# Two transformer blocks on one core: the attention norm through Ln and Exp, lambda as a scalar operand, squares in PSUM, and two buffers for the branches of layer 0

## The chip, the cores and the metric

The kernel runs on one core of a Trainium2 chip. The core's engines run side by side, each through its own queue in order: TensorE (PE, with its weight loads as PEld), VectorE (DVE), ScalarE (ACT), GpSimd (POOL) and SyncE (SP), which here issues most of the DMA transfers. They wait for one another through semaphores. On-chip data lies in SBUF, matmul results in PSUM. The metric is the time of one execution on the device in microseconds (us); lower is better.

## The reference

The first block has two layers, on 512 tokens and 256 tokens of context, with a model width of 2048 and 8 heads. Each layer makes shift, scale and gate vectors from c, projects the modulated tokens by w_in, and runs three kinds of branches: differential attention with a norm of its own, a short convolution, and an average over windows of 2, 4, 8 or 16 tokens less the token itself, which goes through a small matrix. Their concatenation goes through w_out, a residual and a layer norm. A second block (banded attention and a convolution of width 31) follows; the change does not touch it. The part that matters:

```python
def _diff_attn(qb, k_all, v_all, lam):
    s = jnp.einsum('bqhid,bkhid->bhiqk', qb * ATTN_SCALE, k_all)
    p = jax.nn.softmax(s, axis=-1)
    a = p[:, :, 0] - lam * p[:, :, 1]
    return jnp.einsum('bhqk,bkhe->bqhe', a, v_all)

def _diff_subln(o, g, lam_init):
    y = o * lax.rsqrt(jnp.mean(jnp.square(o), axis=-1, keepdims=True) + RMS_EPS) * g * (1.0 - lam_init)
    return y.reshape(o.shape[0], o.shape[1], D_ATTN)

def _short_conv(u, b_gate, c_gate, g, w):
    v = c_gate * u
    vp = jnp.pad(v, ((0, 0), (1, 1), (0, 0)))
    y = vp[:, :T] * w[0] + vp[:, 1:T + 1] * w[1] + vp[:, 2:] * w[2]
    return jax.nn.silu(g) * (b_gate * y)

def _multiscale_pool(u, g, pool_w_l, pool_scale_l):
    ...
    y = jnp.einsum('btgc,gcd->btgd', d, pool_w_l).reshape(B, T, D_POOL) * pool_scale_l
    return jax.nn.silu(g) * y

for l in range(DEPTH):
    sh_l, sc_l, g_l = jnp.split(jax.nn.silu(c) @ w_mod[l] + b_mod[l], 3, axis=-1)
    hl = xl * (1.0 + sc_l[:, None, :]) + sh_l[:, None, :]
    parts_l = jnp.split(hl @ w_in[l], SPLIT_POINTS, axis=-1)
    ...
    xl = _layernorm(DEEPNORM_ALPHA * xl + g_l[:, None, :] * out_l, ln_g[l], ln_b[l])
```

## The kernel before

**Units.** A unit is one block of 128 output columns of w_in against all tokens: 16 steps over the width, each with three matmuls in split precision (a high and a low part of the weights, `whi` and `wlo`, and of the tokens) for the 512 tokens, and as many for the 256 of context. `mm3` (L160 to L163) issues them. SP loads a chunk of weights (`wraw`), ACT rounds it to `whi` (L156), POOL subtracts to get `wlo` (L140). A unit's two results lie in buffers of the PSUM tag `ps_m`, which has four; `ps_s`, `ps_t` and `ps_v` have one each.

**Attention** (`attention`, `attend`). Per head there are four units: Q, K, V and a gate. Q and K are rotated and split, V goes through a copy from PSUM (`vT`, L347 and L348, on ACT) and transposes; the gate becomes SG through `silu2` (a tanh on ACT at L240, a product on DVE at L241). `attend` then goes through groups of 256 queries: three in layer 0 (qp 0 and 1 are the 512 tokens, qp 2 the context), two in layer 1. For each half group and each of the two maps: scores in `ps_s` (L381), maximum (DVE, L386), exp with its sum (ACT, L393), reciprocal of the sum (L395). Then the two maps are combined with lambda (L398 to L401) and transposed through `ps_t` (L408), with a high and a low copy (aTh by ACT, L412, aTl by DVE, L413). The product with V lands in `ps_v` (L418), DVE multiplies it into SG (L422), and for the norm it is squared, split and summed over the partitions by a matmul with ones (L424 to L432). Its result `ms` is copied to `rt` (L435 or L438); after qp 1, for 512 columns, and after qp 2, for 256, Sqrt (ACT, L440), reciprocal (DVE, L445), the product with SG (L446) and the store follow. An activation function needs its table on ACT; where the function changes to one of another table, the built program has an ACT_TABLE_LOAD ahead of it, under the line of that activation.

**Side work.** `dots` (L779 to L815) computes products of modulation weights with c. Every unit advances it by some steps (`along`, `advance`), recorded at a lower priority. A piece `gw` of 512 columns is loaded by SP and used twice, for the tokens and for the context. A product either is one instruction on DVE (L809) or, where `pool_every` picks it, a product on POOL (L805) and a sum on ACT (L806). All of them write their product to the one buffer of the tag `gj`. In layer 0's attention all products go by POOL and ACT; in the branches all 128 go by DVE, with four `gw` buffers.

**Branches** (`conv_tile`, `pool_tile`). Layer 0 runs conv 0, pool 0, conv 1, pool 1, conv 2, pool 2, pool 3, conv 3; the side work runs from pool 0 on. A conv tile takes four units; V and yc are its padded input and its result, stored at L523. A pool tile sums shifted copies of U on POOL (S), takes the mean less the token (dd, L550 and L551), splits dd into dh (ACT, L554) and dl (POOL), and sends them through a matrix into `ps_v`. V and U share the tag "V"; yc, dd and the result y share the tag "yc"; each tag has one buffer.

**Order.** The kernel is written in the Tile framework, which puts in the waits; a scheduler sets the order of the instructions on each engine, on the grounds of data, buffers and priorities. So an edit in one place can move instructions elsewhere.

## Time and profile before

| | us |
|---|---|
| median of 3 runs | 3560.86 (3556.08 to 3561.03) |
| the profiled execution, its own time | 3560.77 |
| its span | 3559.0 |
| PE busy | 3295.3 (93% of the span) |
| DVE busy | 2289.7 (64%) |
| POOL busy | 1956.4 (55%) |
| ACT busy | 1518.4 (43%) |

The profile is of one execution. Its views cut it in several ways. The windows give, for a stretch of time, the busy time of every engine and the mean clock granted to PE, as a share of full speed. The waits give, engine by engine, what it waited for: in front of the arrow the instruction that waits, behind it the one that released it, then the sum in us, how often, and the longest. The timeline lists instructions by start; in brackets stands how long the engine was idle before one and what ended that. The lines group all instructions of one line, engine and shape: count, busy us in all, mean ns of one, then the idle time before them and what ended it. An engine's idle time costs something only where PE, or whatever else sets the end, waits for it.

### The profile page before, as it was taken

The numbers are of one execution on the slowest core, as the hardware profiler recorded it, in microseconds if no ns is written. First come the engines' busy times: TensorE is split into PE (matmuls) and PEld (weight loads), VectorE is DVE, ScalarE is ACT, GpSimd is POOL, SyncE is SP. The second block draws the span as 40 slices with busy tenths as digits, with TensorE's granted clock in tenths as the row PEclk, the third lists the DMA queues.
The fourth block names the chain that finished last, engine by engine and source line by source line (L and its number), as shares of the span: only waits on it lengthen the run. The fifth ranks groups of instructions, "written<-read, shape, count | busy, mean of one in ns | idle before, by whom it ended". The sixth has DMA issues, their size and how long they took to land. (4 is left out here: it accounts for less than half of the span.)

```text
span 3559.0 us, 48355 instructions
## 1 busy us (share of the span) xinstructions
PE 3295.3 (93%) x16850; PEld 2782.2 (78%) x16850; DVE 2289.7 (64%) x3489; ACT 1518.4 (43%) x3181; POOL 1956.4 (55%) x1436
## 2 busy tenths in 40 slices
PE   8898998898998998999999999998999899999997
PEld 7787887787887786778888888877768677787765
DVE  6845555555468548674555564585577799986576
ACT  2256666655431122243666654322445333345333
POOL 2356776665234543256787763587776344444432
PEclk8799999999999999999999999999999999999998
DMA  8744333332245447664555542586775222223575
GB/s 322 284 130 122 104 106 106 98 107 81 68 150 188 143 144 215 188 224 137 154 151 153 162 122 86 204 303 221 230 229 189 74 92 80 86 77 110 180 225 190
DMA packets 274148, 554.70 MB, mean 156 GB/s; under 512 B 30992, under 2 KB 40048, under 8 KB 265712
## 3 DMA queue, kind: packets, MB, share of 16 engines
q1 hardware_dynamic: 271344, 539.04, 47.1%
q0 software_dynamic: 2560, 12.58, 1.7%
q8 instruction: 132, 2.16, 0.3%
q14 instruction: 112, 0.92, 0.1%
HBM read 510.69 MB, written 28.23 MB: 151 GB/s over the span
## 5 line engine op out<-in xcount | busy, mean ns | idle before, releaser
L163 PE MATMUL ps_m<-h,whi 128*128 128x512 f32 (+1 forms) x4736 | 1614.8, 398 | 50.2 <-ACT vT L347 35.1
L140 POOL TENSOR_TENSOR wlo<-wraw,whi 128x512 fp32r<-128x512 f32 x768 | 1119.4, 1474 | 946.6 <-ACT whi L156 882.4
L163 PEld LDWEIGHTS ps_m<-h,whi 128*128 128x128 f32 x4736 | 898.3, 192 | 237.4 <-ACT vT L347 37.4
L156 ACT CAST whi<-wraw 128x512 fp32r<-128x512 f32 x1040 | 607.0, 618 | 874.0 <-DMA wraw<-in_w_out_dram 285.9
L163 PE MATMUL ps_m<-h,wlo 128*128 128x512 f32 (+1 forms) x2368 | 937.5, 396 | 0.6 <-POOL wlo L140 0.6
L163 PE MATMUL ps_m<-hc,whi 128*128 128x256 f32 x2048 | 557.0, 283 | 0.9 <-DVE SG L241 0.9
L805 POOL TENSOR_TENSOR gpr<-gw,gv 128x512 f32<-128x512 f32 x320 | 426.0, 1331 | 220.3 <-ACT gpr L806 149.4
L163 PEld LDWEIGHTS ps_m<-h,wlo 128*128 128x128 f32 x2368 | 453.7, 192 | 94.5 <-POOL wlo L140 2.0
L163 PEld LDWEIGHTS ps_m<-hc,whi 128*128 128x128 f32 x2048 | 383.1, 190 | 4.6 <-DVE SG L241 1.4
L140 DVE TENSOR_TENSOR wlo<-wraw,whi 128x512 fp32r<-128x512 f32 x272 | 239.2, 893 | 202.9 <-ACT whi L156 202.6
L806 ACT ACTIVATE gpr<-gpr 128x512 f32<-128x512 f32 x320 | 201.8, 631 | 271.9 <-POOL gpr L805 270.0
L163 PE MATMUL ps_m<-hc,wlo 128*128 128x256 f32 x1024 | 289.1, 282 | 0.0
L989 DVE SCALAR_TENSOR_TENSOR acc<-gu,pack,acc 128x511 f32<-128x511 f32 (+24 forms) x240 | 230.3, 972 | 5.4
L609 PE MATMUL ps_m<-wlo,y 128*128 128x512 f32 x512 | 205.5, 402 | 18.1 <-POOL wlo L140 10.9
L809 DVE SCALAR_TENSOR_TENSOR gpr<-gw,gv 128x512 f32<-128x512 f32 x232 | 214.3, 924 | 8.7 <-DMA gw<-in_w_ada_dram 1.6
L386 DVE TENSOR_REDUCE nb<-ps_s 128x1 f32<-128x768 f32 (+1 forms) x160 | 135.2, 845 | 114.5 <-PE ps_s L381 113.3
L610 PE MATMUL ps_m<-whi,y 128*128 128x512 f32 x512 | 202.6, 397 | 2.5 <-DVE y L140 2.3
L163 PEld LDWEIGHTS ps_m<-hc,wlo 128*128 128x128 f32 x1024 | 194.5, 190 | 0.8
L608 PE MATMUL ps_m<-whi,y 128*128 128x512 f32 x512 | 181.8, 397 | 6.5 <-ACT whi L156 5.4
L413 DVE TENSOR_TENSOR aTl<-ps_t,aTh 128x384 fp32r<-128x384 f32 (+1 forms) x144 | 77.6, 539 | 166.8 <-ACT aTh L412 166.4
L282 DVE SCALAR_TENSOR_TENSOR wm<-wm,ca 128x2048 f32<-128x2048 f32 x50 | 128.8, 2575 | 21.0 <-DMA wm<-in_w_ada_dram 11.6
L381 PE MATMUL ps_s<-K,Q 128*128 128x384 f32 x576 | 133.9, 346 | 8.3 <-ACT E L393 6.6
(351 smaller groups left out, 5217.9 us busy)
## 6 DMA issues: line engine op xcount, KB each, us to landing
wraw<-in_w_in_dram SPq DMA_DIRECT2D x640, 256.0 KB, 2.9
wraw<-in_w_out_dram SPq DMA_DIRECT2D x384, 256.0 KB, 3.4
wm<-in_w_mod_dram SPq DMA_DIRECT2D x48, 1024.0 KB, 6.0
gw<-in_w_mod_dram SPq DMA_DIRECT2D x192, 256.0 KB, 3.4
gw<-in_w_ada_dram SPq DMA_DIRECT2D x136, 256.0 KB, 3.3
wm<-in_w_ada_dram SPq DMA_DIRECT2D x14, 1024.0 KB, 5.9
K<-K POOLq DMA_DIRECT2D x32, 384.0 KB, 5.4
gv<-in_cc_dram SPq DMA_DIRECT2D x40, 256.0 KB, 3.6
```

Source lines behind the costliest of these rows:

```text
L140: eng.tensor_tensor(lo, src, hi.bitcast(F32), op=ALU.subtract)
L156: nc.scalar.copy(hi[:, sl], raw)
L163: nc.tensor.matmul(ps, w, mv[part], start=(first and p == 0), stop=(last and p == 2))
L381: nc.tensor.matmul(o, Qm[:, q0:q0 + 128], kp[:, c * ncol:(c + 1) * ncol], start=i == 0, stop=i == 1)
L386: nc.vector.reduce_max(nb, sv, axis=AX.XY, negate=True)
L608: nc.tensor.matmul(ps, yh, hi[:, sl], start=(k == 0), stop=False)
L609: nc.tensor.matmul(ps, yh, lo[:, sl], start=False, stop=False)
L610: nc.tensor.matmul(ps, yl, hi[:, sl], start=False, stop=(k == KT - 1))
L805: nc.gpsimd.tensor_tensor(pr, w, t, op=ALU.mult)
L806: nc.scalar.activation(pr, pr, AF.Copy, scale=scale, accum_out=part[v][:, i:i + 1])
L809: nc.vector.scalar_tensor_tensor(junk, w, scale, t, op0=ALU.mult, op1=ALU.mult, accum_out=part[v][:, i:i + 1])
L989: nc.vector.scalar_tensor_tensor(A[:, s:], U[:, :NL - s], wj(i), A[:, s:], op0=ALU.mult, op1=ALU.add)
```

## The change

- The product of the reciprocal sum with minus lambda, one column, takes lambda as a scalar operand (`tensor_scalar`) in place of a second tensor.
- The squares `o2` go to the second half of the PSUM bank that holds `o`, in place of an SBUF tile.
- The norm: ACT reads `ms` from PSUM with Ln (scale 8 and the same bias), into `rt`, for each group; then Exp with scale -0.5 follows where Sqrt was, for 512 or 256 columns. Copy, Sqrt and DVE's reciprocal are gone; the product with SG stays.
- In layer 0 (l = 0) the tags "V" and "yc" have two buffers (`2 - l`); in layer 1 they keep one.
- The dots in the branches of layer 0 have three `gw` buffers in place of four, and every third product goes by POOL and ACT, in all 43 of 128.

```diff
@@ -395,7 +395,7 @@
                     nc.vector.reciprocal(r, d)
                     es.append(e)
                     ds.append(r)
-                nc.vector.tensor_tensor(ds[1], ds[1], neglam[l], op=ALU.mult)
+                nc.vector.tensor_scalar(ds[1], ds[1], neglam[l], None, op0=ALU.mult)
                 E0, E1 = es
                 nc.vector.tensor_scalar(E0, E0, ds[0], None, op0=ALU.mult)
                 nc.vector.scalar_tensor_tensor(E0, E1, ds[1], E0, op0=ALU.mult, op1=ALU.add)
@@ -420,7 +420,7 @@
                     )
             y = SG[:, qp * 256:(qp + 1) * 256]
             nc.vector.scalar_tensor_tensor(y, o, subg[l], y, op0=ALU.mult, op1=ALU.mult)
-            o2 = ap_.tile([128, 256], F32, name="o2", tag="o2", bufs=1)
+            o2 = ov[:, 256:]
             nc.scalar.square(o2, o)
             o2h = ap_.tile([128, 256], F32R, name="o2h", tag="o2h", bufs=1)
             o2l = ap_.tile([128, 256], F32R, name="o2l", tag="o2l", bufs=1)
@@ -430,20 +430,18 @@
             ms = msv[:, :256]
             nc.tensor.matmul(ms, ones_r, o2h, start=True, stop=False)
             nc.tensor.matmul(ms, ones_r, o2l, start=False, stop=True)
+            if qp != 1:
+                rt = ap_.tile([128, 512], F32, name="rt", tag="rt", bufs=1)
+            r = slice(256, 512) if qp == 1 else slice(0, 256)
+            nc.scalar.activation(rt[:, r], ms, AF.Ln, bias=eps_t, scale=8.0)
             if qp == 0:
-                rt = ap_.tile([128, 512], F32, name="rt", tag="rt", bufs=1)
-                nc.scalar.copy(rt[:, :256], ms)
                 continue
-            r = slice(256, 512) if qp == 1 else slice(0, 256)
-            nc.scalar.copy(rt[:, r], ms)
             n = 512 if qp == 1 else 256
-            nc.scalar.activation(rt[:, :n], rt[:, :n], AF.Sqrt, bias=eps_t, scale=8.0)
+            nc.scalar.activation(rt[:, :n], rt[:, :n], AF.Exp, scale=-0.5)
             for i in range(n // 256):
                 q0 = (0, 256)[i] if qp == 1 else 512
-                ri = rt[:, i * 256:(i + 1) * 256]
                 y = SG[:, q0:q0 + 256]
-                nc.vector.reciprocal(ri, ri)
-                nc.vector.tensor_tensor(y, y, ri, op=ALU.mult)
+                nc.vector.tensor_tensor(y, y, rt[:, i * 256:(i + 1) * 256], op=ALU.mult)
             o = 0 if qp == 1 else 512
             nc.sync.dma_start(Yd[4 + h][:, o:o + n], SG[:, o:o + n])
 
@@ -497,9 +495,9 @@
         uu = xa.tile([128, T], F32, name="uu", tag="uu", bufs=1)
         for o, vo, n in seqs:
             nc.scalar.copy(uu[:, o:o + n], pt(u, o))
-        V = xa.tile([128, T + 4], F32, name="V", tag="V", bufs=1)
+        V = xa.tile([128, T + 4], F32, name="V", tag="V", bufs=2 - l)
         u = unit(w, 8 + j, H, cx)
-        yc = xa.tile([128, T], F32, name="yc", tag="yc", bufs=1)
+        yc = xa.tile([128, T], F32, name="yc", tag="yc", bufs=2 - l)
         for o, vo, n in seqs:
             nc.vector.memset(V[:, vo:vo + 1], 0.0)
             nc.vector.memset(V[:, vo + n + 1:vo + n + 2], 0.0)
@@ -527,7 +525,7 @@
         seqs = ((0, 8, NL), (NL, NL + 24, NCX))[:1 if cx is None else 2]
         pt = lambda u, o: u.lat if o == 0 else u.cx
         W = T + 16 * len(seqs)
-        U = xa.tile([128, T + 32], F32, name="U", tag="V", bufs=1)
+        U = xa.tile([128, T + 32], F32, name="U", tag="V", bufs=2 - l)
         nc.gpsimd.memset(U, 0.0)
         if (l, g) in EARLY:
             for o, vo, n in seqs:
@@ -544,7 +542,7 @@
             s2 = xp.tile([128, T + 32], F32, name="S2", tag="pgr" if step in (1, 4) else "dh", bufs=1)
             nc.gpsimd.tensor_tensor(s2[:, :wd], s[:, :wd], s[:, step:step + wd], op=ALU.add)
             s, step = s2, step * 2
-        dd = xa.tile([128, T], F32, name="dd", tag="yc", bufs=1)
+        dd = xa.tile([128, T], F32, name="dd", tag="yc", bufs=2 - l)
         for o, vo, n in seqs:
             f = vo - win // 2
             nc.gpsimd.tensor_tensor(dd[:, o:o + n], s[:, f:f + n], rc[:, o:o + n], op=ALU.mult)
@@ -560,7 +558,7 @@
         nc.vector.tensor_copy(ph, pw)
         sub_lo(pl, pw, ph, nc.vector)
         gate = early_gate(xp, g) if l == 0 else unit(w, 52 + g, H, cx)
-        y = xa.tile([128, T], F32, name="yp", tag="yc", bufs=1)
+        y = xa.tile([128, T], F32, name="yp", tag="yc", bufs=2 - l)
         for o, vo, n in seqs:
             th = xp.tile([128, NL], F32, name="th", tag="th", bufs=2)
             silu2(th[:, :n], gate[:, o:o + n] if l == 0 else pt(gate, o), th[:, :n])
@@ -861,7 +859,7 @@
     mod_row("c0", 32, "c0")
     Y = early_y(0, 6)
     with pool("dots1", R) as gp:
-        along(mod_dots1(gp, 1, 4, 20, 4), 6)
+        along(mod_dots1(gp, 1, 4, 20, 3, 3), 6)
         branch(xp, xp, 0, H, Hc, NT, steps[1:])
         finish()
     es_h.close()
```

The built program has 83 ACT_TABLE_LOADs, 51 before. The 16660 matmuls are the same; on PE they stand in another order within the two attentions, and the pool tiles' matmuls (L163, `ps_v<-dh`) of pool 0 and pool 1 stand some 110 matmuls earlier.

ACT in layer 0, the sixth head, from the second group's square-mean (`ps_v`) to the copies of the value unit's PSUM (`vT`); `gpr` are the dots, `K` the split of the keys, `rsh` the gate's tanh. Before:

```order
L438 COPY rt<-ps_v 128x256
L806 ACTIVATE gpr,gpart<-gpr 128x512
L440 ACT_TABLE_LOAD
L440 ACTIVATE rt<-rt,eps_t 128x512
L341 CAST K_6244<-qr 64x768
L393 ACT_TABLE_LOAD
L393 ACTIVATE ps_s,dn<-ps_s,nb 128x256
L156 CAST whi<-wraw 128x512 x2
L240 ACTIVATE rsh<-ps_m 128x512
L806 ACTIVATE gpr,gpart<-gpr 128x512
L347 COPY vT<-ps_m 128x512
```

The same place of the changed program (line numbers are those of the changed file):

```order
L436 ACT_TABLE_LOAD
L436 ACTIVATE rt<-ps_v,eps_t 128x256
L440 ACT_TABLE_LOAD
L440 ACTIVATE rt<-rt 128x512
L341 CAST K_6219<-qr 64x768
L393 ACTIVATE ps_s,dn<-ps_s,nb 128x256
L804 ACTIVATE gpr,gpart<-gpr 128x512
L347 COPY vT<-ps_m 128x512
L348 COPY vT<-ps_m 128x256
L156 CAST whi<-wraw 128x512 x2
L240 ACTIVATE rsh<-ps_m 128x512
```

The load of the softmax's exp is gone from here, and two casts and the tanh stand behind the copies of vT.

ACT in the same head, its first group (qp 0), where the square-mean's copy stands ahead of a softmax exp. Before:

```order
L427 CAST o2h<-o_5723 128x256
L806 ACTIVATE gpr,gpart<-gpr 128x512
L412 CAST aTh<-ps_t 128x3x128
L806 ACTIVATE gpr,gpart<-gpr 128x512
L435 COPY rt<-ps_v 128x256
L393 ACTIVATE E_5781,dn<-ps_s,nb 128x768
```

In the changed program:

```order
L427 CAST o2h<-ps_v 128x256
L156 CAST whi<-wraw 128x512 x2
L804 ACTIVATE gpr,gpart<-gpr 128x512
L337 COPY qr<-ps_m 128x256
L412 CAST aTh<-ps_t 128x3x128
L436 ACT_TABLE_LOAD
L436 ACTIVATE rt<-ps_v,eps_t 128x256
L393 ACT_TABLE_LOAD
L393 ACTIVATE E_5760,dn<-ps_s,nb 128x768
```

Two loads stand around the activation that took the copy's place; the casts of weights have moved ahead of it.

POOL in the branches of layer 0, at pool 0: `U` is the padded input, S its sum over the window, `dd` the mean less the token; `wlo` is the low part of weights, `y` a part of the loads for w_out. Before:

```order
L531 MEMSET U 128x800
L140 TENSOR_TENSOR y_7_9764<-yraw_9765,y_7_9764 128x512
L140 TENSOR_TENSOR wlo<-wraw,whi 128x512
L545 TENSOR_TENSOR S_9788<-U 128x799
L140 TENSOR_TENSOR wlo<-wraw,whi 128x512
L140 TENSOR_TENSOR y_9_9774<-yraw_9775,y_9_9774 128x512
L140 TENSOR_TENSOR wlo<-wraw,whi 128x512 x6
L550 TENSOR_TENSOR dd<-S_9788,rc 128x512
L550 TENSOR_TENSOR dd<-S_9788,rc 128x256
L551 TENSOR_TENSOR dd<-dd,U 128x512
```

In the changed program:

```order
L529 MEMSET U 128x800
L140 TENSOR_TENSOR y_5_9714<-yraw_9715,y_5_9714 128x512
L543 TENSOR_TENSOR S_9748<-U 128x799
L548 TENSOR_TENSOR dd<-S_9748,rc 128x512
L548 TENSOR_TENSOR dd<-S_9748,rc 128x256
L140 TENSOR_TENSOR y_7_9724<-yraw_9725,y_7_9724 128x512
L549 TENSOR_TENSOR dd<-dd,U 128x512
L140 TENSOR_TENSOR wlo<-wraw,whi 128x512 x2
L549 TENSOR_TENSOR dd<-dd,U 128x256
L803 TENSOR_TENSOR gpr<-gw,gv_9905 128x512
```

`dd` follows S at once, ahead of the `wlo` that stood before it, and the products of the dots begin behind it.

## Rows read from the trace of the kernel before

**Rows 1.** Stretches: length; busy us of PE, PEld, DVE, ACT, POOL; clock; DMA

```profile
250.00:960.00 710.00, 639.33 (x3728) 563.41 (x3728) 386.53 (x617) 420.64 (x973) 451.60 (x353) 0.95 0.35 101
960.00:1300.00 340.00, 318.33 (x1790) 276.15 (x1789) 204.16 (x416) 77.96 (x147) 146.17 (x107) 0.96 0.46 144
1600.00:2200.00 600.00, 590.60 (x3248) 513.38 (x3247) 322.12 (x480) 336.98 (x746) 421.61 (x332) 1.00 0.49 140
```

**Rows 2.** Waits of PE, 250 to 960 us: total us, times, longest

```profile
PE ps_m L163 <- ACT vT L347: 35.1, 7, 7.8
PE ps_t L408 <- DVE aTl L413: 13.2, 6, 5.7
PE ps_m L163 <- ACT qr L323: 11.7, 4, 4.8
```

**Rows 3.** Waits of PE, 960 to 1300 us

```profile
PE ps_v L163 <- ACT dh L554: 19.6, 2, 10.3
```

**Rows 4.** Timeline of ACT and PE, sixth head of layer 0: start, duration (us)

```profile
705.15 0.37 ACT L438 COPY rt<-ps_v 128x256 f32<-128x256 f32 x1 [2.43 <-PE ps_v L432]
...
706.17 1.28 ACT L440 ACT_TABLE_LOAD   x1
707.46 0.72 ACT L440 ACTIVATE rt<-rt,eps_t 128x512 f32<-128x512 f32 x1
708.21 0.83 ACT L341 CAST K<-qr 64x768 fp32r<-64x768 f32 x1
709.05 1.28 ACT L393 ACT_TABLE_LOAD   x1
710.35 0.45 ACT L393 ACTIVATE ps_s<-ps_s,nb 128x256 f32<-128x256 f32 x1
...
713.05 0.57 ACT L347 COPY vT<-ps_m 128x512 f32<-128x512 f32 x1
...
713.67 1.22 PE L163 MATMUL ps_m<-h,whi 128*128 128x512 f32 x2 [6.46 <-ACT vT L347]
```

**Rows 5.** Timeline: a first group in layer 0; a load ahead of a wait

```profile
778.33 0.90 ACT L393 ACTIVATE E<-ps_s,nb 128x768 f32<-128x768 f32 x1
...
781.80 0.51 PE L381 MATMUL ps_s<-K,Q 128*128 128x384 f32 x2
...
3241.81 1.28 ACT L1124 ACT_TABLE_LOAD   x1
3245.86 0.69 ACT L1124 ACTIVATE rt<-ps_m,eps_t 128x512 f32<-128x512 f32 x1 [2.77 <-PE ps_m L1108]
```

**Rows 6.** Lines over the span (L809: 960 to 1300): count, busy us, mean ns, idle before

```profile
L440 ACT ACT_TABLE_LOAD x24 | 30.8, 1283 | 0.4
L445 DVE RECIPROCAL rt<-rt 128x256 f32<-128x256 f32 x40 | 67.8, 1729 | 51.8 <-ACT rt L440 51.8
L398 DVE TENSOR_TENSOR rd<-rd,neglam 128x1 f32<-128x1 f32 x80 | 34.9, 436 | 2.5
L413 DVE TENSOR_TENSOR aTl<-ps_t,aTh 128x384 fp32r<-128x384 f32 (+1 forms) x144 | 77.6, 539 | 166.8 <-ACT aTh L412 166.4
L805 POOL TENSOR_TENSOR gpr<-gw,gv 128x512 f32<-128x512 f32 x320 | 426.0, 1331 | 220.3 <-ACT gpr L806 149.4 <-DMA gw<-in_w_ada_dram 26.4 <-ACT whi L156 14.8
L806 ACT ACTIVATE gpr<-gpr 128x512 f32<-128x512 f32 x320 | 201.8, 631 | 271.9 <-POOL gpr L805 270.0 <-DVE rd L398 1.2
L806 ACT ACTIVATION_READ_ACCUMULATOR gpr<-gpr 128x1 f32 x320 | 60.0, 188 | 0.0
L809 DVE SCALAR_TENSOR_TENSOR gpr<-gw,gv 128x512 f32<-128x512 f32 x128 | 120.2, 939 | 4.4 <-DMA gw<-in_w_mod_dram 1.1
```

**Rows 7.** Timeline of pool 0 and pool 1, which PE waits for

```profile
1069.84 1.69 POOL L550 TENSOR_TENSOR dd<-S,rc 128x512 f32<-128x512 f32 x2 [14.15 <-DMA yd<-yc]
...
1080.80 0.79 PE L163 MATMUL ps_v<-dh,ph 128*128 128x512 f32 x1 [9.27 <-ACT dh L554]
...
1153.21 1.09 POOL L550 TENSOR_TENSOR dd<-S,rc 128x512 f32<-128x512 f32 x1 [16.10 <-DVE gpr L809]
```

## The prediction

> **What bounds the kernel now.** The page's first part is read first: TensorE (PE) is busy 93% of the span, no other engine over 64%. So a microsecond counts only if PE stands idle or runs at a lower clock; busy time on ACT, DVE and POOL matters only where PE waits for it. I then cut the span into the three stages that the change touches [rows 1]. Layer 0's attention (250 to 960 us) has 710.00 us with 639.33 of PE work: 70.7 us idle, at a granted clock of 0.95 of full, so about 0.05 x 710 = 35 us more go to running slowly. Layer 0's branches (960 to 1300) have 21.7 us idle and 0.04 x 340 = 13.6 us of lost clock. Layer 1's attention (1600 to 2200) has 9.4 us idle at clock 1.00. So up to 106 us stand to be won in the first stage, 35 in the second and nearly nothing in the third, though the same norm runs in both attentions.
>
> The waits of PE by what ended them say what the idle time is [rows 2]. In layer 0's attention 35.1 us are seven waits for `vT<-ps_m` (L347): the value unit's PSUM is copied out by ACT, and PE's next unit has no free ps_m buffer before that. Another 13.2 and 11.7 us are waits for aTl (DVE) and for the copy of qr (ACT). In the branches 19.6 of 21.7 us are two waits for dh, the pooled difference [rows 3].
>
> **Attention: the wait for vT.** The sixth head shows why ACT is late [rows 4]. ACT is in order. From the second group's square-mean to the copy of vT it runs the copy L438 (705.15), a dot's accumulate, the table load and Sqrt (1.28 and 0.72), half of K, a second table load for the softmax's exp (1.28), that exp, two casts of weights, a tanh and another accumulate; vT starts at 713.05 and PE resumes at 713.67 after 6.46 us without work. The change replaces copy and Sqrt by Ln and Exp, and keeps two loads in this place: before Ln, and before Exp. What shrinks is the part behind the square-mean. The load before Ln depends on nothing and Ln waits for one thing, the square-mean; where this kernel already has such a pair, at L1124, the load runs 2.77 us ahead of the activation that waits for PE [rows 5]. So the first load goes into the 2.43 us for which ACT waits now, and no third switch is needed for the softmax, since Exp stays loaded. In the new order the two casts and the tanh also stand behind vT in this head. Its chain becomes Ln 0.4, load 1.28, Exp 0.72, K 0.83, exp 0.45, accumulate 0.63 and 0.2 each for reading out two sums [rows 4, 6]: 4.7 us where 7.9 stood. I walked the seven heads that wait in both orders with these durations, and took for each what PE still has to do before it needs the buffer. What ACT lacks sums to 34.6 us before, against the 35.1 measured, and to 12.7 after: **22 us** less. One head (the fourth) keeps its order and its wait. If the load carried the wait too, each head lost 1.28: 10 us less, which is my lower bound, 12; the upper is all 35.
>
> **Attention: the later waits.** The 24.9 us for aTl and qr come from DVE and ACT being late in the third group, where DVE waits for Sqrt and then takes 1.73 us for each reciprocal, 40 in all, having idled 51.8 us for them [rows 6]. The reciprocals go. Against that, the gate SG and its store now wait for Exp, 0.5 to 0.7 us after the load, and the next head's gate for the store. I take half, **13 us**, between nothing and all 24.9.
>
> **The mid-head loads.** The first group (qp 0) had only a copy. Now it has a load, Ln, a load, in front of a softmax exp: 2 x 1.28 = 2.57 us more, 16 times, 41 us of ACT; those are the 32 loads that the new order has above the old (83 against 51). In the head shown, the exp is done at 779.23 and PE comes to the K-Q product that overwrites its bank at 781.80: 2.57 us of slack [rows 5]. With the first load running ahead, 1.3 us are added and half the slack is left; without it none. Over eight heads I take 1 us each, **8 us** back (0 to 20). In layer 1 it has the same slack and the Sqrt pair goes as above: I take 0, from -5 to +10.
>
> The 1283 ns are the whole price in this trace: Sqrt starts 0.01 us after its load [rows 4], and all 24 loads have 0.4 us of idle time before them [rows 6]. The Trainium skill ("ScalarE: Activation LUTs", section "What ACT_TABLE_LOAD costs") adds a drain of about 1380 ns, 2.66 us for a switch; by it the 32 loads would be 85 us of ACT, overrun the slack in each head and end at 3561 + 85 - 24 = 3622. The rows above do not show that drain.
>
> **Clock.** Half clock follows the waits: I let the 35 us shrink with the idle time. Idle goes from 71 to 71 - 22 - 13 + 8 = 44, so the loss goes from 35 to 35 x 44/71 = 22. Attention 0: 27 + 13 = **40 us**.
>
> **Small parts.** The product with lambda (L398, 80 x 436 ns) is 35 us of DVE; by a scalar it costs between nothing and the same. It lies between the softmax sums and E, which DVE has long done when PE reads it except at the waits counted above: 0. The squares in PSUM change only where three instructions read and write; L413 already subtracts with a PSUM source, at 539 ns for 384 columns [rows 6], so the three should cost about what they do, between 0.2 us less and 0.2 us more for each of 40 groups, 8 us either way at worst. The bank is now read until o2l is done, but its next user, the square-mean, needs o2l anyway: 0.
>
> **Branches.** In pool 0, POOL's dd waits 14.15 us for the store of yc, because both share one buffer, and PE gets dh 9.27 us late [rows 7]. The second, 16.10 us on POOL in pool 1, is said to be for a dot on DVE (L809): the buffer was freed by DVE work that stands behind dots. With two buffers dd can start when S is there, which POOL had ready over 14 us before; in the new order dd of pool 0 follows S at once. Both waits go, if nothing else is late. But the dots move: every third of 128 goes to POOL and ACT, 43 in all, through the one gj buffer that DVE's products also use, so the three engines take turns: 1.33 + 0.63 + 0.19 + 2 x 0.94 = 4.03 us for three, 43 x 4.03 = 173 us [rows 6]. DVE's other work in the window is 204 - 120 = 84 us. Four of the 17 units come before the dots, so they have about 13/17 x 340 = 260 us for 173 + 84 = 257: it fits, and better the more of the other work overlaps POOL's and ACT's turns, but the fourth gw buffer is missing as a cushion. The pool products, now standing some 110 matmuls earlier in PE's order, have little spare. I leave 5 us of new waits: idle 21.7 - 19.6 + 5 = 7, clock 13.6 x 7/21.7 = 4.4, so 14.6 + 9.2 = **24 us** (bounds 33 and -16: the dots run 11 us over the end, with 5 of clock, an estimate if none of the 84 us is hidden and the first turn starts late).
>
> **Sum.** -40 - 24 + 0 = -64 from the profiled execution's 3560.77, which stands 0.1 us from the median: **3497 us**.
>
> **Rivals.**
> 1. *The mid-head loads land on PE (slower).* The place is qp 0 of each of the 16 heads, the price 2.57 us each, 41 us; it decides wherever PE reaches the next K-Q product less than 2.6 us after the exp's old end. The row shown is just at that point; for it speak 16 more switches on an engine that is already late in layer 0, against it that layer 1 waits 9.4 us in 600. With the waits for vT unchanged and the branches won: 3561 + 41 - 24 = 3578.
> 2. *The dots take the branches' gain.* The three engines in lockstep end late, and w_out waits for them: 3561 - 40 + 16 = 3537. For it: 257 us of work in 260; against: DVE has a third less of the dots.
> 3. *The attention's waits only change names.* PE starts earlier, finds weights (whi, wlo) or Q not ready, and idles as long: 3561 - 24 = 3537. For it: ACT and POOL take turns at the dots all through this stage; against: PE loses only 9.4 us in layer 1 with the same code.
> 4. *One set of tables serves Ln and Exp*, so that no loads would be needed between them: the loads saved would be worth up to 24 x 1.28 = 31 us more, 3466. The new order has a load before each of the 40 Ln and before the Exp or softmax behind it, so it has no chance here. The Trainium skill ("ScalarE: Activation LUTs", section "Table sets: the hidden batching unit") lists a set with both; the built order does not use it.
>
> **How the numbers follow.** Forecast 0.55, rival 1 0.08, rival 2 0.17, rival 3 0.15, rivals 2 and 3 together, 3561 + 0 to 16, 0.05. About 0.2%, 7 us, is what a measurement tells from no change. Slower then holds rival 1 and a little of the last: 0.09; same 0.05; faster 0.86. Low end: idle down to 36 and clock to 10 in attention 0 (35 + 25 = 60), 33 in the branches, 5 in layer 1: 3561 - 98 = 3463. High end: rivals 2 and 3 with 8 us on top, 3545.
>
> **What would show it.** Right: waits for vT below 20 us and for aTl and qr below 15 in layer 0; no wait for dh; clock 0.97 or more in 250 to 910; loads 83, of which Ln's run before their wait. Wrong: new waits of PE on E (L393) in both attentions (rival 1), on gpr, gw or at the start of w_out (rival 2), on whi, wlo or Q (rival 3); or half clock that stays though the waits shrink.

## The result, and the profile of the changed kernel

The changed kernel takes 3503.44 us (median of four runs, 3500.04 to 3506.32), against 3560.86 before. The ratio is 0.984, with an interval of 0.9826 to 0.9852: **57 us faster, where 64 were forecast** (3497 us; range 3463 to 3545). The profiled execution took 3500.04 us, with a span of 3498.3.

Both traces hold 16850 matmul records (not the program's 16660), as many at each line before as after, so the same work can be compared by count: the start of the 1200th, the 5200th and so on in each trace cuts the program into stages that hold nearly the same work. The table goes from the start of the first matmul to the start of the last. Span against span the difference is 60.7 us.

| stage (matmuls by count) | before, us | after, us | difference | forecast |
|---|---|---|---|---|
| from the first matmul, no edit in it (0 to 1200) | 242.2 | 239.4 | -2.8 | 0 |
| layer 0's attention (1200 to 5200) | 754.4 | 705.5 | -48.9 | -40 |
| layer 0's branches (5200 to 6700) | 292.1 | 276.7 | -15.4 | -24 |
| layer 0's w_out and norm (6700 to 8000) | 330.9 | 334.2 | +3.3 | 0 |
| layer 1 up to its w_out (8000 to 12400) | 884.1 | 885.0 | +0.9 | 0 |
| the rest, to the last matmul (from 12400) | 1032.7 | 1035.0 | +2.3 | 0 |

The first stage comes before any edit, and over all traces of this study it takes 239 to 249 us. So a few us in one stage of one execution mean nothing; the total has its interval from several runs. The branches are as loose: in the seven kernels below and here that have both edits in the branches and the dots as in the change, they take 275.6 to 285.7 us, and the change's 276.7 lies at the low end.

The page of the changed kernel first. PE's busy time fell by 21 us for the same matmuls, about what the clock gave back in the attention (below); DVE's by 130.

```profile
span 3498.3 us, 48421 instructions
PE 3274.6 (94%) x16850; PEld 2765.5 (79%) x16850; DVE 2159.9 (62%) x3361; ACT 1589.5 (45%) x3301; POOL 2006.2 (57%) x1480
```

The windows of the three stages, cut where they now lie (length, then busy us of PE, PEld, DVE, ACT and POOL, granted clock, DMA), answer to [rows 1]:

```profile
250.00:910.00 660.00, 624.87 (x3716) 553.19 (x3716) 323.87 (x590) 433.08 (x977) 446.58 (x351) 0.98 0.38 108
910.00:1235.00 325.00, 315.44 (x1793) 273.95 (x1792) 184.74 (x326) 110.39 (x237) 205.20 (x149) 0.99 0.49 147
1540.00:2140.00 600.00, 583.86 (x3211) 506.10 (x3210) 273.94 (x461) 352.82 (x756) 414.76 (x329) 1.00 0.49 139
```

In layer 0's attention PE is idle for 35.1 us where it was for 70.7, and the clock is 0.98 where it was 0.95: 0.02 x 660 = 13 us lost where 35 were. By the clock's own records, half clock (1.2 GHz) was granted there in ten stretches, 65 us in all, before, and in three, 27 us, after. In layer 1 it is idle for 16.1 of 600 us where it was for 9.4.

The waits of PE in the same three stages (total us, times, longest), one fence with a gap for each stage, answer to [rows 2, 3]:

```profile
PE ps_t L408 <- DVE E L401: 16.0, 5, 8.1
PE ps_m L163 <- ACT vT L347: 6.8, 3, 3.5
PE ps_s L381 <- ACT E L393: 4.2, 4, 1.7
...
PE ps_t L408 <- DVE aTl L413: 2.0, 3, 1.4
...
PE ps_v L163 <- DVE yp L567: 7.9, 3, 5.7
...
PE ps_s L381 <- ACT E L393: 9.4, 7, 2.4
```

The wait for vT fell from 35.1 to 6.8 us. The wait for aTl fell from 13.2 to 2.0, and that for qr (11.7) is gone. Another now stands at the head of the list: transposes that wait for E, the combined softmax, 16.0 us in five waits, where it was 1.5. In the branches no wait for dh is left; 7.9 us in three waits are for yp, the read of the pool tile's PSUM by DVE, where it was 1.0.

The sixth head again, on ACT, with the last matmul of the square-mean and the first after vT on PE (start and duration in us, idle time in brackets), answers to [rows 4]:

```profile
679.07 1.28 ACT L436 ACT_TABLE_LOAD   x1
679.33 0.28 PE L432 MATMUL ps_v<-o2l,ones_r 128*128 128x256 f32 x1
680.37 0.48 ACT L436 ACTIVATE rt<-ps_v,eps_t 128x256 f32<-128x256 f32 x1
680.86 1.28 ACT L440 ACT_TABLE_LOAD   x1
682.16 0.63 ACT L440 ACTIVATE rt<-rt 128x512 f32<-128x512 f32 x1
682.82 0.84 ACT L341 CAST K<-qr 64x768 fp32r<-64x768 f32 x1
683.95 0.45 ACT L393 ACTIVATE ps_s<-ps_s,nb 128x256 f32<-128x256 f32 x1 [0.30 <-DVE nb L386]
...
684.52 0.61 ACT L804 ACTIVATE gpr<-gpr 128x512 f32<-128x512 f32 x1
...
685.13 0.56 ACT L347 COPY vT<-ps_m 128x512 f32<-128x512 f32 x1
...
685.75 0.73 PE L163 MATMUL ps_m<-h,whi 128*128 128x512 f32 x2 [1.35 <-ACT vT L347]
```

From Ln's start to the copy of vT there are 4.76 us, where 7.90 stood from the copy L438 (705.15 to 713.05). The forecast was 4.7. But ACT no longer waits here for the square-mean: it comes to the load straight from a dot's sum, and the square-mean is done at 679.61, while the load runs. Counted from that point vT starts 5.52 us later, where it was 7.93 before (705.12 to 713.05). PE waits 1.35 us for vT in this head, where it waited 6.46.

### The profile page after: what moved, and what is told of

It reads as the page before. It is cut to its first block, busy times and chain, and to the rows that moved or that the text cites. A ratio compares the mean times of both kernels' runs of the same rounds, so it can differ in the third digit from the quotient of the medians.

```text
span 3498.3 us, 48421 instructions
## 1 busy us (share of the span) xinstructions
PE 3274.6 (94%) x16850; PEld 2765.5 (79%) x16850; DVE 2159.9 (62%) x3361; ACT 1589.5 (45%) x3301; POOL 2006.2 (57%) x1480
## 5 line engine op out<-in xcount | busy, mean ns | idle before, releaser
L163 PE MATMUL ps_m<-h,whi 128*128 128x512 f32 (+1 forms) x4736 | 1601.1, 395 | 10.0 <-ACT vT L347 6.8
L163 PEld LDWEIGHTS ps_m<-h,whi 128*128 128x128 f32 x4736 | 889.7, 190 | 193.7 <-ACT vT L347 8.2
L163 PE MATMUL ps_m<-h,wlo 128*128 128x512 f32 (+1 forms) x2368 | 931.7, 394 | 0.0
L803 POOL TENSOR_TENSOR gpr<-gw,gv 128x512 f32<-128x512 f32 x364 | 484.5, 1331 | 293.6 <-ACT gpr L804 169.6
L163 PE MATMUL ps_m<-hc,whi 128*128 128x256 f32 x2048 | 560.9, 282 | 0.0
L163 PEld LDWEIGHTS ps_m<-h,wlo 128*128 128x128 f32 x2368 | 449.4, 190 | 91.6
L804 ACT ACTIVATE gpr<-gpr 128x512 f32<-128x512 f32 x364 | 230.0, 632 | 384.1 <-POOL gpr L803 383.0
L163 PEld LDWEIGHTS ps_m<-hc,whi 128*128 128x128 f32 x2048 | 383.1, 189 | 1.8
L163 PE MATMUL ps_m<-hc,wlo 128*128 128x256 f32 x1024 | 288.8, 282 | 0.0
L807 DVE SCALAR_TENSOR_TENSOR gpr<-gw,gv 128x512 f32<-128x512 f32 x188 | 184.3, 980 | 83.2 <-ACT gpr L804 78.2
L163 PEld LDWEIGHTS ps_m<-hc,wlo 128*128 128x128 f32 x1024 | 194.0, 189 | 1.0
L413 DVE TENSOR_TENSOR aTl<-ps_t,aTh 128x384 fp32r<-128x384 f32 (+1 forms) x144 | 77.9, 541 | 182.1 <-ACT aTh L412 181.7
L607 PEld LDWEIGHTS ps_m<-wlo,y 128*128 128x128 f32 x512 | 97.1, 190 | 55.6 <-POOL wlo L140 18.9
```

The lines of the kernel that those rows point to most:

```text
L163: nc.tensor.matmul(ps, w, mv[part], start=(first and p == 0), stop=(last and p == 2))
L607: nc.tensor.matmul(ps, yh, lo[:, sl], start=False, stop=False)
L803: nc.gpsimd.tensor_tensor(pr, w, t, op=ALU.mult)
L804: nc.scalar.activation(pr, pr, AF.Copy, scale=scale, accum_out=part[v][:, i:i + 1])
L807: nc.vector.scalar_tensor_tensor(junk, w, scale, t, op0=ALU.mult, op1=ALU.mult, accum_out=part[v][:, i:i + 1])
```

## The experiments

All ratios are against the kernel before, run beside it on the same chip, with the interval in brackets; us are the ratio's difference from 1, times 3561. For the stages I use the cuts of the table above, from one trace each.

**The norm alone.** The edit: the lines of the norm as in the change, on the kernel before; o2 stays in SBUF, lambda a tensor, the branches as they were.

```diff
-            nc.scalar.activation(rt[:, :n], rt[:, :n], AF.Sqrt, bias=eps_t, scale=8.0)
+            nc.scalar.activation(rt[:, r], ms, AF.Ln, bias=eps_t, scale=8.0)
...
+            nc.scalar.activation(rt[:, :n], rt[:, :n], AF.Exp, scale=-0.5)
...
-                nc.vector.reciprocal(ri, ri)
```

> The kernel before with the norm alone through Ln and Exp. Theory (the shorter chain on ACT and the missing reciprocals free PE in layer 0's attention): that attention loses 35 to 47 us, its waits for vT fall from 35 us below 12, layer 1's attention gains 0 to 10, the whole is 3515 to 3530. Rival (the gain of the attention comes from the cheaper subtraction of the squares and the cheaper product with lambda on DVE): 3550 to 3565 here.

Measured: 3523.66 us, ratio 0.9894 (0.988 to 0.9908), -38 us. Layer 0's attention takes 703.7 us, 50.7 less than before: as much as in the whole change. The waits for vT are 10.4 us. So the norm makes the attention's gain, and the rival, that the subtraction and the product with lambda make it, is out. Which part of the norm does it (no Sqrt, no reciprocals on DVE, another order on ACT) this run doesn't say. The branches take 296.9 (+4.8), and layer 1 894.1 (+10.0).

**Lambda and the squares alone.**

```diff
-                nc.vector.tensor_tensor(ds[1], ds[1], neglam[l], op=ALU.mult)
+                nc.vector.tensor_scalar(ds[1], ds[1], neglam[l], None, op0=ALU.mult)
...
-            o2 = ap_.tile([128, 256], F32, name="o2", tag="o2", bufs=1)
+            o2 = ov[:, 256:]
```

> The kernel before with lambda as a scalar operand and the squares in PSUM, nothing else. Theory (these lie beside PE's work): within 5 us of before, 3555 to 3566. Rival (they carry what the norm alone and the branches alone leave unexplained of the whole change, 3561 - 3503 - 40 - 7 = 11 us): 3545 to 3553, with the gain in layer 0's attention.

Measured: 3560.69 us, ratio 1.0006 (0.9996 to 1.0015): no change. The forecast was right in the total and wrong in its reason. Layer 0's attention is 17.9 us shorter (736.5), and the branches give back 15.4 (307.5), 12.0 of it in longer waits for dh, which were 19.6 us before [rows 3]:

```profile
PE ps_v L163 <- ACT dh L554: 31.6, 2, 16.6
```

PE comes to the branches earlier and waits there for the same late work: they begin at 983.1 us in place of 998.7, and the 6700th matmul, their end, starts at 1290.7 in both traces. A gain ahead of a stage that another engine paces is not a gain.

**Both edits in the branches.** Two buffers, every third product of the dots on POOL and ACT, three gw buffers.

```diff
-        dd = xa.tile([128, T], F32, name="dd", tag="yc", bufs=1)
+        dd = xa.tile([128, T], F32, name="dd", tag="yc", bufs=2 - l)
...
-        along(mod_dots1(gp, 1, 4, 20, 4), 6)
+        along(mod_dots1(gp, 1, 4, 20, 3, 3), 6)
```

> The kernel before with two buffers in the branches of layer 0 and the dots moved, the attention as it was. Theory (both waits of PE for dh were for a buffer): the branches lose 15 to 25 us, the whole is 3536 to 3546, and the attention is as before. Rival (the branches gain only what the attention hands on in time): under 8 us, above 3553.

Measured: 3556.51 us, ratio 0.998 (0.9968 to 0.9991), -7 us. The branches take 284.8 us (-7.3): the rival's figures. PE waits no more for dh, but 11.9 us for yp.

**The buffers without the dots.** As above, with the dots all on DVE; they have three gw buffers in place of four here too.

```diff
-        along(mod_dots1(gp, 1, 4, 20, 4), 6)
+        along(mod_dots1(gp, 1, 4, 20, 3), 6)
```

> The kernel before with two buffers in the branches alone; the fourth gw buffer goes too, since two buffers leave no room for it; all dots stay on DVE. Theory (the waits for dh were waits for a buffer): most of the gain of both edits together is here, 10 to 20 us, 3541 to 3551. Rival (DVE, with the dots ahead of the work that frees the buffer, makes dh late): under 5 us, above 3556.

Measured: 3569.04 us, ratio 1.0018 (1.0009 to 1.0027): slower, by 6 us. The waits for dh are gone, and two for yp stand in their place:

```profile
PE ps_v L163 <- DVE yp L569: 24.3, 2, 14.4
```

PE had the first part of pool 0's product in the one `ps_v` bank at 1058.6, and the next part had to wait until DVE had read it. On DVE that read (L569) stands behind a row of dots, of which the first and the last are shown here, with the tanh products (L241) that it also needs:

```profile
1059.08 0.08 DVE L809 DVE_READ_ACCUMULATOR gpr<-gw,gv 128x1 f32 x1
1060.86 0.76 DVE L809 SCALAR_TENSOR_TENSOR gpr<-gw,gv 128x512 f32<-128x512 f32 x1 [1.70 <-DMA gw<-in_w_mod_dram]
...
1077.58 0.69 DVE L809 SCALAR_TENSOR_TENSOR gpr<-gw,gv 128x512 f32<-128x512 f32 x1
1078.19 0.08 DVE L809 DVE_READ_ACCUMULATOR gpr<-gw,gv 128x1 f32 x1
1078.19 0.42 DVE L241 SCALAR_TENSOR_TENSOR th<-th,pgr 128x256 f32<-128x256 f32 x1
1078.53 0.74 DVE L569 SCALAR_TENSOR_TENSOR yp<-ps_v,psc,th 128x512 f32<-128x512 f32 x1
```

So the shared buffer was the last of two limits that lay close together. The one behind it is DVE's order: the dots ahead of what PE needs. The fourth gw buffer, which is missing too, has some part in it: between 1000 and 1330 us the dots on DVE wait 9.8 us for gw, where it was 1.1 before [rows 6]; that part was not taken out.

**The dots alone.** Two buffers taken out again, the dots as in the change.

```diff
-        along(mod_dots1(gp, 1, 4, 20, 4), 6)
+        along(mod_dots1(gp, 1, 4, 20, 3, 3), 6)
```

> The kernel before with the dots alone moved: every third on POOL and ACT, three gw buffers, one buffer in the branches. Theory (buffers make the gain): dd still waits for the store of yc, and the turns that three engines take through one buffer cost time: 3555 to 3575. Rival (DVE makes dh late): 10 to 20 us less, 3541 to 3551.

Measured: 3556.91 us, ratio 0.9987 (0.9975 to 0.9999), -5 us: in the first theory's range, at its low end. The waits for dh are 16.9 us in four pieces, where they were 19.6 in two. Neither edit alone removes the wait: the buffer without relief for DVE moves it to yp, the relief without the buffer leaves it at dh. In the total this run and the one with both edits (-7) can't be told apart, and in the branches they differ by 3.4 us (288.2 and 284.8). So what the buffers add on top of the relief of DVE isn't shown.

**The change without its branches, and without lambda and squares.** These two take one part out of the whole change.

```diff
-        dd = xa.tile([128, T], F32, name="dd", tag="yc", bufs=2 - l)
+        dd = xa.tile([128, T], F32, name="dd", tag="yc", bufs=1)
...
-        along(mod_dots1(gp, 1, 4, 20, 3, 3), 6)
+        along(mod_dots1(gp, 1, 4, 20, 4), 6)
```

> The changed kernel without its edits in the branches (one buffer, all dots on DVE, four gw buffers). Theory (the parts are not additive: what PE gains in the attention is eaten in the branches while DVE there holds all dots ahead of the work PE waits for): the branches are 5 to 20 us longer than in the changed kernel, with waits for dh of 20 us and more; the whole is 3515 to 3530. Rival (the parts add: the branches are worth 7 us as alone): 3507 to 3513.

Measured: 3518.49 us, ratio 0.9879 (0.9857 to 0.9901), -43 us. The branches take 290.5 us, 13.8 more than in the change, with 18.5 us of waits for dh. That is the theory's range, though its waits for dh were to be 20 us or more. On top of the other parts the edits in the branches are worth 14 us; alone they were worth 7.

```diff
-                nc.vector.tensor_scalar(ds[1], ds[1], neglam[l], None, op0=ALU.mult)
+                nc.vector.tensor_tensor(ds[1], ds[1], neglam[l], op=ALU.mult)
...
-            o2 = ov[:, 256:]
+            o2 = ap_.tile([128, 256], F32, name="o2", tag="o2", bufs=1)
```

> The changed kernel without lambda as a scalar and without the squares in PSUM. Theory (they are worth nothing alone, but with the branches mended what DVE saves in the attention, 0.45 us for each subtraction and 0.22 for each product, is kept): 3508 to 3520, layer 0's attention and layer 1's 4 us or more longer than in the changed kernel. Rival (they are worth nothing here either): 3500 to 3507.

Measured: 3510.27 us, ratio 0.9858 (0.9835 to 0.988), -51 us; so lambda and squares bring some 7 us on top of the rest, but the intervals overlap. Of the two places expected, layer 0's attention shows nothing (700.9 us, 4.6 less than in the change); layer 1 does: 893.3 us with the squares in SBUF and lambda a tensor, 885.0 in the change. The pair of the norm alone (894.1) and of norm with lambda and squares (885.9) shows the same 8 us. The branches differ by 9 (285.7), where the wait for yp is 15.1 us, but that is within what kernels with these edits show.

**Fewer table loads: the first group's copy kept.** The second group's square-mean is copied too, and one Ln over 512 columns follows it.

```diff
-            nc.scalar.activation(rt[:, r], ms, AF.Ln, bias=eps_t, scale=8.0)
+            n = 512 if qp == 1 else 256
             if qp == 0:
+                nc.scalar.copy(rt[:, r], ms)
                 continue
-            n = 512 if qp == 1 else 256
+            if qp == 1:
+                nc.scalar.copy(rt[:, r], ms)
+                ms = rt
+            nc.scalar.activation(rt[:, :n], ms[:, :n], AF.Ln, bias=eps_t, scale=8.0)
```

> The changed kernel with the copy of the first group's square-mean kept and one Ln for both groups after the second: 32 loads fewer than in the change. Theory (the loads ahead of a softmax exp cost PE a little in each head, most in layer 1): layer 1's attention gets 5 to 12 us back, layer 0's up to 8, the waits of PE for E fall to 5 us or less in layer 1, and the whole is 3485 to 3498. Rival (those loads are hidden, and layer 1 is longer because of the order the scheduler chose): 3500 to 3510, waits for E as they are.

Measured: 3519.51 us, ratio 0.9888 (0.9874 to 0.9902), -40 us: 17 us worse than the change, with 24 loads at Ln in place of 40. Both expectations fell. Layer 1 takes 887.3 us, no less than in the change (885.0). Layer 0's attention takes 717.1 (705.5) and the branches 283.5 (276.7), in a trace of an execution of 3532 us, 13 above this kernel's median; its first stage, without an edit, is 9.6 us longer too. The sixth head, on ACT and PE:

```profile
696.76 0.36 ACT L441 COPY rt<-ps_v 128x256 f32<-128x256 f32 x1
...
698.00 0.45 ACT L393 ACTIVATE ps_s<-ps_s,nb 128x256 f32<-128x256 f32 x1
...
699.29 1.28 ACT L443 ACT_TABLE_LOAD   x1
700.59 0.72 ACT L443 ACTIVATE rt<-rt,eps_t 128x512 f32<-128x512 f32 x1
700.97 0.69 PE L408 MATMUL ps_t<-ident,E 128*128 128x128 f32 x2 [5.35 <-DVE E L401]
701.21 0.56 ACT L347 COPY vT<-ps_m 128x512 f32<-128x512 f32 x1
```

The square-mean's copy must come first, and so the load for Ln stands behind the square-mean again, as with Sqrt. But PE doesn't wait for it here: vT starts 5.84 us after the square-mean's last matmul, where it was 5.52 in the change, and the 5.35 us for which PE stands in this head are for E, whose exp (698.00) is ahead of the load. Over the attention, PE's waits for vT are 9.0 us (6.8 in the change), those for E 16.4 (16.0), and 3.5 are for the gate (SG); in the branches one of 7.3 us, for a row of modulation that DVE copies, is new. So no row shows that the load behind the copy makes the 17 us. What makes them stays open.

**The norm once a head.** Copies for all groups, then one Ln, one Exp, one product: 35 loads in all in place of 83.

```diff
...
+            nc.scalar.copy(rt[:, qp * 256:(qp + 1) * 256], ms)
+            if (qp + 1) * 256 < T:
                 continue
...
+            nc.scalar.activation(rt[:, :T], rt[:, :T], AF.Ln, bias=eps_t, scale=8.0)
+            nc.scalar.activation(rt[:, :T], rt[:, :T], AF.Exp, scale=-0.5)
+            nc.vector.tensor_tensor(SG, SG, rt[:, :T], op=ALU.mult)
```

> The changed kernel with the norm once a head: the square-means of all groups are copied to SBUF, and one Ln, one Exp and one product follow after the last group; two loads a head in place of six in layer 0 and four in layer 1. Theory (what is left of the waits in layer 0, 16 us for E and 7 for vT, are loads on ACT's way to exp and vT): these waits fall below 8 us, layer 1 gains 5 to 12, the whole is 3475 to 3495. Rival (SG has one buffer, and its late product and store hold back the next head's gate): waits of PE on the gate's PSUM appear, and the whole is 3505 or more.

Measured: 3504.35 us, ratio 0.985 (0.9832 to 0.9868): the same as the change, in neither of the two ranges, though all square-means are copied before Ln here. The waits for E are down from 16.0 to 2.0 us, but vT has 10.2, aTl 7.9, and the gate (SG) 3.1. Layer 1 takes 885.6 us, so the loads in its heads cost it nothing that shows. With 48 loads fewer nothing is gained; the late gate may take back what they bring.

**The dots' products over their own inputs.** In layer 0's attention alone.

```diff
-                        pr = xp.tile([128, 512], F32, name="gpr", tag="gj", bufs=1)
+                        pr = w if pool_every == 1 and v else xp.tile([128, 512], F32, name="gpr", tag="gj", bufs=1)
```

> The changed kernel with every second product of the dots in layer 0's attention (and in no other place) written over its own gw buffer, so that POOL need not wait for ACT's sum before its next product. Theory (what is left of the waits there comes from ACT standing at a dot's sum until POOL has its product, 134 us in all, with exp and vT queued behind): that wait falls below 80 us, the waits of PE in the stage fall by 8 us or more, and the whole is 3480 to 3496. Rival (the table loads are what is left): 3500 to 3506.

Measured: 3536.49 us, ratio 0.9933 (0.9912 to 0.9954), 33 us worse than the change; layer 0's attention takes 735.9 us. ACT's wait for POOL on the line's sums splits into 70.7 us (gpr) and 42.3 (gw) and falls only from 133.9 to 113.0. POOL runs the dots sooner and waits elsewhere: for whi on ACT 157.9 us, where it was 59.2, and for gw 45.2. PE's waits for E grow to 29.6 us. The theory fell.

**Another PSUM bank for the pool tiles' context part.**

```diff
-            ps = ps_v()
+            ps = ps_v() if o == 0 else ps_t()
```

> The changed kernel with the context part of each pool tile in another PSUM bank than the part of the 512 tokens. Theory (what is left in the branches, 7.9 us of waits for yp, comes from both parts sharing one bank, which DVE frees late): these waits are gone, the branches lose 5 to 12 us, the whole is 3492 to 3499. Rival (DVE is late as such, and the next reader waits for the same work): 3500 to 3506, the wait turns up elsewhere.

Measured: 3501.38 us, ratio 0.9837 (0.982 to 0.9854): no change against the changed kernel. The waits for yp are gone, and one for dh of 8.1 us has come; the rival was right.

**A product buffer of its own for DVE's dots**, on top of that bank.

```diff
-                    junk = xp.tile([128, 512], F32, name="gpr", tag="gj", bufs=1)
+                    if pool_every == 3:
+                        junk = xp.tile([128, 512], BF16, name="gpd", tag="gjd", bufs=1)
...
```

> The changed kernel with a product buffer of its own (bf16, 1 KB) for DVE's dots in the branches of layer 0, so that DVE does not take turns with POOL and ACT, and with the context part of the pool tiles in another PSUM bank, as in the run before. Theory (what is left in the branches is the turns: DVE waits 78 us there for ACT's sums, with th and yp behind): DVE's wait for ACT's sums is gone, the waits of PE for dh and yp fall from 8 us below 3, the branches lose 5 to 12 us against the run with the bank alone, and the whole is 3488 to 3497. Rival (the loads of gw with three buffers set the pace of the dots, whoever does them): DVE waits for gw instead, 3498 to 3506.

Measured: 3540.92 us, ratio 0.9941 (0.9924 to 0.9958): 37 us worse than the bank alone. The branches take 311.1 us. DVE no longer takes turns, and waits for the loads of gw; PE waits for what stands behind. The waits from 950 to 1300 us (the first line is one of DVE, the others are of PE):

```profile
DVE gpd L810 <- DMA gw<-in_w_mod_dram: 44.0, 26, 3.6
...
PE ps_m L163 <- DVE th L241: 12.0, 2, 8.2
...
PE ps_m L163 <- DVE yc L513: 9.7, 2, 6.0
...
PE ps_m L163 <- DVE V L504: 4.2, 1, 4.2
```

The rival's mechanism was right, its price far too small. That the turns with POOL and ACT had held the dots back, so that the conv tiles' work came through between them, would explain it, but is only argued: the scheduler's order changed with the buffer too, and what each of the two costs was not taken apart.

No kernel of the study is clearly faster than the change.

## Why the prediction was right, and where it was not

**The total.** Forecast -64, measured -57 (median). It is inside the range, and so near by luck: two errors of 9 us in opposite directions met, as the attention gave more than forecast and the branches less.

**The wait for vT: right in direction, not in the way.** 12.7 us were forecast to be left, 6.8 were. The forecast's step was that the first load goes into the time for which ACT waits for the square-mean. The rows before and after show how much waiting there was, in front of the copies and then in front of Ln:

```profile
L438 ACT COPY rt<-ps_v 128x256 f32<-128x256 f32 x24 | 8.8, 366 | 18.9 <-PE ps_v L432 18.7
L435 ACT COPY rt<-ps_v 128x256 f32<-128x256 f32 x16 | 5.8, 363 | 1.9 <-PE ps_v L432 1.9
```

```profile
L436 ACT ACT_TABLE_LOAD x40 | 51.3, 1283 | 0.7
L440 ACT ACT_TABLE_LOAD x24 | 30.8, 1283 | 0.4
L436 ACT ACTIVATE rt<-ps_v,eps_t 128x256 f32<-128x256 f32 x40 | 19.0, 476 | 8.6 <-PE ps_v L432 8.0
```

Where ACT still waits, the load has indeed run ahead, as forecast; but of the 8.6 us, 8.0 lie at three places (945, 962 and 2204 us), none of them ahead of a vT that PE waits for. Of the 21 loads at Ln between 250 and 910 us, 14 begin after the square-mean's last matmul has ended, six begin before that and end behind it, and one is over before; of their 27 us some 3.5 run ahead. So most of these loads stand in ACT's way, like the ones before. In the sixth head the room where ACT waited is filled with work that the new order moved up (casts of weights, sums of dots), and what stands behind the square-mean is shorter, by two casts, the tanh, a dot's sum and the softmax's load, against part of Ln's.

What makes the gain within the norm is not shown. In the kernels with the new norm and the attention's dots as they were, with 35, 51 or 83 loads and with the copies or without, the waits for vT are 6.2 to 10.4 us and layer 0's attention takes 701 to 717. What they share, against the kernel before, is that Sqrt and DVE's 40 reciprocals are gone, and no run takes out one of these alone. And part of the wait went to another name, as the next step shows: for vT and E together PE waited 36.6 us before and waits 22.8 now, 13.8 less where 22 were forecast for vT.

**The later waits: right in kind, too small.** 24.9 us were to become 12; for aTl and qr 2.0 are left. But 14.5 us of waits for E came, against 1.5 before. Two of the waits for E take 8.1 and 5.9 us, in two heads, and around both ACT is the busy engine, with 8.99 of 10 and 7.90 of 8 us (the fourth of the busy times in the windows):

```profile
590.00:600.00 10.00, 1.94 (x12) 1.64 (x11) 3.32 (x7) 8.99 (x19) 6.47 (x6) 0.80 0.59 158
769.00:777.00 8.00, 2.12 (x11) 1.70 (x10) 4.24 (x8) 7.90 (x15) 4.56 (x5) 0.78 0.56 152
```

There Ln, a load and Exp stand ahead of the softmax's exp, but so do sums of dots, a cast of the keys and, in the first, casts of weights and a tanh. This is the forecast's third rival in a small way. With fewer loads the time doesn't fall (the norm once a head), so which of these makes E late stays open.

**The mid-head loads: the size was off.** I gave back 8 us in layer 0 and 0 in layer 1. PE's waits for E at L393 are 4.2 us in layer 0 and 9.4 in layer 1, where they were 1.7 and 4.9: rival 1 in a small way, some 7 us of its 41. Layer 1 as a whole is 0.9 us longer, and with 48 loads fewer nothing was gained.

**Clock: the proportion was too mild.** I let the loss shrink with the idle time, to 22 us; idle halved (70.7 to 35.1) and the loss fell to 13. The half clock lies around the long waits, and those went first: before, waits of up to 7.8 us stood in seven heads, with ten stretches at half clock; after, two over 5 us are left, and two of the three stretches (6.8 us each) lie around these. The third, 13.7 us from 319.6 on, has three waits of 1 to 2 us.

**Small parts: the step failed, hidden by the total.** I gave lambda and the squares 0, and bounded the subtraction of the squares by 0.2 us either way. It went from 867 to 421 ns, the product with lambda from 436 to 214. Alone they shorten layer 0's attention by 18 us and are then eaten by the branches; with the rest they are worth 5 to 7, in intervals that overlap. The forecast took the subtraction's price from another one with a PSUM source (L413) and did not set the 867 ns beside it; 867 and 436 are means over two very different cases, told below.

**Branches: the cause was wrong.** "Both waits go, if nothing else is late": with the buffers alone they go and come back as 24.3 us for yp, because DVE holds dots ahead of what the pool tile needs. The waiting row [rows 7] named a DMA for pool 0, and the store of conv 0's yc was indeed late, but because DVE had yc behind dots. In the kernel before, the tanh for yc's last product is done at 1053.85 us; DVE runs dots until it multiplies the tanh at 1064.71, and the store leaves behind yc's last product:

```profile
1052.99 0.86 ACT L240 ACTIVATE th<-ps_m 128x512 f32<-128x512 f32 x2
...
1064.71 1.01 DVE L241 SCALAR_TENSOR_TENSOR th<-th,ps_m 128x512 f32<-128x512 f32 x2
...
1066.25 1.02 DVE L520 SCALAR_TENSOR_TENSOR yc<-yc,th 128x512 f32<-128x512 f32 x2
...
1067.30 0.33 SPq L523 DMA_DIRECT2D yd<-yc  x1
```

The forecast booked the dots' move as a cost (turns through one buffer, 173 us), but the relief of DVE is what the gain can't do without: the buffers without it lose 6 us. What the buffers add to it in the whole change is not shown. The turns themselves did no harm that shows: in the kernel without them the branches were 35 us longer (311.1 against 275.6 with the bank alone). Of the 24 us forecast, 15.4 came in the profile, and the changed kernel without these edits is 14 us slower.

**Parts don't add.** Alone: norm -38, branches -7, lambda and squares +2, together -43. All at once: -57. The norm's gain is partly lost in the branches (+4.8) and layer 1 (+10.0) unless the other two are there.

## What to carry to other kernels

A wait in the old profile is no room to book for a new instruction: the new order can fill it with other work, so look after the change whether the engine still waits at that place. When a wait names a buffer, ask what is late behind the buffer's last user: a second buffer only moves the wait if an engine's queue holds unurgent work ahead of it. Measure parts in the company of the others, since a stage paced by another engine eats what the stage before it wins.

## What the runs showed of the hardware

**Two SBUF operands on DVE.** The subtraction o2l, by tile, in the kernel before and then in the changed one (durations min/median/max in ns). It has the same shape; only o2 moved to PSUM.

```profile
L140 DVE TENSOR_TENSOR o2l<-o,o2h x40: 411/905/1533, 301.5 to 2255.6; 128x256 fp32r<-128x256 f32 x40
```

```profile
L140 DVE TENSOR_TENSOR o2l<-ps_v,o2h x40: 394/425/426, 297.3 to 2199.4; 128x256 fp32r<-128x256 f32 x40
```

From SBUF alone it takes 411 ns at best and 1533 at worst; with one operand in PSUM it is never slowed. The product with lambda goes from 96 to 1771 ns as two tensors, and from 202 to 217 with a scalar operand. POOL is busy for 55% of the span, and the traces show that the slow ones are those beside it. Before, the 13 subtractions that overlap no instruction of POOL, or only one's edge, took 411 to 426 ns; of the 27 others five took 416 to 516 and 22 took 885 to 1533. After, 28 of the 40 overlap one, and none took more than 426. Before, all 43 products that took 239 ns or more overlap one too, and the 26 that overlap nothing took at most 163. The Trainium skill ("GPSIMD Engine Reference", section "1. Specifications") says that GpSimd shares its SBUF interfaces with VectorE and that they get in each other's way when a DVE instruction has two SBUF inputs; these durations agree with that, though no run here takes POOL away.

**The table load.** It took 1283 ns at L436 and L440 alike, as before at L440, with 0.02 us to the activation behind it where nothing else was waited for (680.86 + 1.28 to 682.16). The Trainium skill ("ScalarE: Activation LUTs", section "What ACT_TABLE_LOAD costs") adds a drain of some 1380 ns to a switch; no trace here shows it. The Trainium skill ("ScalarE: Activation LUTs", section "Table sets: the hidden batching unit") lists a set with both exp and ln, by which an Exp behind Ln would need no load of its own; the built program loads one before each.
